# Strided attention on one core: a two-bank normalisation split over three engines, and sums taken one group ahead

## Chip, core, metric

One core of a Trainium2 chip. The metric is the device time of one execution in microseconds (us), the median of several executions. "Span" is the length of the profiled execution; the measured time is about 1.8 us longer. Ratios between kernels are the mean time of one kernel's fast runs over that of the other's of the same rounds, so they are not quite the ratios of the medians that are quoted.

## The reference

Each of 96 heads has 1024 queries of 64 numbers and attends to 16 fixed keys (every 64th position).

```python
for i in range(seq):                                   # cut
    attend_positions = np.arange(0, seq, stride)       # 16 keys
    scores = einsum('bhqd,bhkd->bhqk', q, k) * scale
    weights = np.exp(scores - max); weights /= weights.sum(-1)
    result[:, :, i] = einsum('bhqk,bhkd->bhqd', weights, v)
```

Q is 25 MB in and the result 25 MB out; the arithmetic is small.

## The kernel before

Work goes in 24 groups of 4 heads, 1 MB of Q and 1 MB of output each. GpSimd casts Q to bf16, VectorE transposes it, TensorE makes scores, ScalarE exponentiates them, TensorE makes sums and outputs, VectorE multiplies the outputs by the reciprocal sums, and the DMA queue stores. TensorE's matmuls and VectorE's instructions run in the order of the source, as the trace of before shows (in the group from 72.37 us: sums at 72.37, outputs at 72.87, scores at 73.68, outputs at 74.71). The parts that matter:

```python
def transpose(g):
    nc.vector.transpose(qt[g].bitcast(I32), qb[g].bitcast(I32))

def scores(g):                       # 4 matmuls of 512 columns, then exp
    ...
    for a in range(2):
        nc.scalar.activation(out=..., in_=sc[64*a:64*a+64]..., func=AF.Exp, scale=scale)

def sums(g):                         # 8 weight loads, 8 matmuls of 4 columns
    for i in range(8):
        nc.tensor.matmul(sm[:, :, i], lhsT=wt[g][:, i], rhs=s_sel, ...)
    nc.vector.reciprocal(rec[g], sm...)

def outputs(g, c):                   # c = 0..3: 2 matmuls, one 128x512 multiply
    ...
    nc.vector.tensor_tensor(out=out_sb[g][:, :, 4*c:4*c+4], in0=ps, in1=rec[g]..., op=ALU.mult)

for g in range(NG):
    transpose(g + 2)
    sums(g)
    outputs(g, 0); outputs(g, 1)
    scores(g + 1)
    outputs(g, 2); outputs(g, 3)
    values(g + 2); cast(g + 3)       # GpSimd
    if g in (2, 4): keys(g // 2)     # prepares the keys of 8 more groups
    store(g)
    load(g + 10)
```

Note where the transpose stands: first in group g, for the scores of group g+2, which TensorE reaches only in group g+1.

The softmax here doesn't subtract the row's maximum and nothing guards it: scores larger than these inputs give would overflow.

## Time and profile before

| | before |
|---|---|
| time, median of 4 | 129.65 us |
| VectorE busy | 85% of the span, 97% from 60 us on |
| time per group, steady | 3.97 us |
| DMA | 401 GB/s mean, about 420 in a full stretch |
| last store issued | 120.0 us of 127.7 |

From the page of before: the first line gives the busy time of each engine (PE is TensorE's matmuls, DVE VectorE, ACT ScalarE, POOL GpSimd), the second the busy tenths of the DMA engines in 40 equal slices of the span, the third the volume.

```profile
PE 73.3 (57%) x508; PEld 38.6 (30%) x508; DVE 109.2 (85%) x170; ACT 39.6 (31%) x55; POOL 66.7 (52%) x69
DMA  2999989898998998989989999999999999999981
HBM read 25.95 MB, written 25.17 MB: 400 GB/s over the span
```

From the table of stretches of before: start and end in us, length, busy time (instructions) of each engine, granted TensorE clock (PEclk, the share of full speed that the profile records; 1.00 is full), DMA share, GB/s.

```profile
core 0: us, PE busy (x) PEld busy (x) DVE busy (x) ACT busy (x) POOL busy (x), PEclk, DMA share, GB/s
60.00:70.00 10.00, 5.84 (x55) 3.45 (x55) 9.72 (x17) 4.10 (x6) 7.51 (x6) 1.00 1.01 424
90.00:100.00 10.00, 6.28 (x47) 3.24 (x45) 9.73 (x16) 4.16 (x6) 5.42 (x5) 0.91 1.01 424
```

DMA is full and VectorE is nearly full at once. The groups of instructions of before that VectorE works through (count, total busy us, mean ns of one, idle before and what ended it):

```profile
L254 DVE TENSOR_TENSOR out_sb<-o_ps,rec 128x512 f32<-128x512 f32 x96 | 59.9, 685 | 4.8 <-PE o_ps L249 2.6
L211 DVE STREAM_TRANSPOSE qt<-qb 128x1024 int32<-128x1024 int32 x24 | 29.7, 1237 | 1.6 <-POOL qb L207 1.6
L242 DVE RECIPROCAL rec<-sm 128x32 f32<-128x32 f32 x24 | 7.8, 326 | 0.3 <-PE sm L238 0.3
```

And one group in the timeline of before (start us, duration us, instruction):

```profile
70.55 1.24 DVE L211 STREAM_TRANSPOSE qt<-qb 128x1024 int32<-128x1024 int32 x1
...
71.71 0.32 DVE L242 RECIPROCAL rec<-sm 128x32 f32<-128x32 f32 x1
...
72.12 2.49 DVE L254 TENSOR_TENSOR out_sb<-o_ps,rec 128x512 f32<-128x512 f32 x4
...
73.68 1.24 PE L218 MATMUL sc<-qt,k_t 128*128 128x512 bf16 x4
...
74.52 1.24 DVE L211 STREAM_TRANSPOSE qt<-qb 128x1024 int32<-128x1024 int32 x1
```

VectorE goes from transpose to transpose with hardly a gap in 3.97 us. The transpose ends at 71.79, and the next scores start only at 73.68: those scores don't even use it yet.

### The profile page before, as it was taken

The page shows a single profiled execution, that of the slowest core. Times are in us where ns is not written, and L with a number is a line of the kernel's source. Part 1 is how long each engine was busy: PE and PEld are TensorE (multiplying, and loading weights), DVE is VectorE, ACT ScalarE, POOL GpSimd, SP SyncE. Part 2 cuts the span into 40 slices and gives each one's busy share as a digit, 9 for nine tenths or more (in the row PEclk, how much of TensorE's full clock was granted, in tenths as well). Part 3 has the DMA queues.
Part 4 walks back from the last instruction along what each step waited for, and adds up shares of the span by engine and source line. Part 5 has one row for each costly group of instructions (what it writes and reads, how often), then busy time and mean ns, then how long its engine had stood idle before and what let it go on. Part 6 is the DMA issues. An engine that isn't in the chain of part 4 may idle for free. (4 is left out here: it accounts for less than half of the span.)

```text
span 127.7 us, 1518 instructions
## 1 busy us (share of the span) xinstructions
PE 73.3 (57%) x508; PEld 38.6 (30%) x508; DVE 109.2 (85%) x170; ACT 39.6 (31%) x55; POOL 66.7 (52%) x69
## 2 busy tenths in 40 slices
PE   0006767974476097866675579755567776674000
PEld 0003233441433063333342234432234323342000
DVE  6997468999979987899999999999999999999500
ACT  3003404224244134344424440444431344323000
POOL 8980499675217605387767635787555727000000
PEclk9999999999779855599999965799998559999555
DMA  2999989898998998989989999999999999999981
GB/s 70 380 322 459 482 339 482 349 482 359 462 472 336 503 400 377 505 346 431 493 344 439 454 385 436 441 408 452 426 398 464 385 421 431 426 416 428 421 372 46
DMA packets 7913, 51.23 MB, mean 401 GB/s; under 512 B 3872, under 2 KB 3872, under 8 KB 3872
## 3 DMA queue, kind: packets, MB, share of 16 engines
q1 hardware_dynamic: 7904, 51.12, 96.8%
q8 instruction: 4, 0.07, 0.2%
q14 instruction: 5, 0.04, 0.1%
HBM read 25.95 MB, written 25.17 MB: 400 GB/s over the span
## 5 line engine op out<-in xcount | busy, mean ns | idle before, releaser
L254 DVE TENSOR_TENSOR out_sb<-o_ps,rec 128x512 f32<-128x512 f32 x96 | 59.9, 685 | 4.8 <-PE o_ps L249 2.6
L229 ACT ACTIVATE w<-sc 64x512 bf16<-64x512 f32 x48 | 35.1, 732 | 60.0 <-PE sc L218 56.7
L207 POOL CAST qb<-qn 128x2048 bf16<-128x2048 f32 x24 | 45.5, 1898 | 0.4 <-DMA qn<-in_Q_dram 0.4
L249 PE MATMUL o_ps<-vb,w 128*128 128x256 bf16 x192 | 38.0, 321 | 2.4 <-DVE out_sb L254 1.4
L199 POOL TENSOR_TENSOR vb<-mask,v_rep 128x256 bf16<-128x256 bf16 x24 | 16.1, 670 | 40.3 <-PE o_ps L249 35.4
L218 PE MATMUL sc<-qt,k_t 128*128 128x512 bf16 x96 | 32.7, 472 | 1.5 <-DVE qt L211 1.2
L211 DVE STREAM_TRANSPOSE qt<-qb 128x1024 int32<-128x1024 int32 x24 | 29.7, 1237 | 1.6 <-POOL qb L207 1.6
L249 PEld LDWEIGHTS <-w 128*128 128x128 bf16 x192 | 19.3, 110 | 16.2 <-issue 8.6
L238 PE MATMUL sm<-s_sel,w 128*128 128x4 bf16 x192 | 8.7, 167 | 22.1 <-ACT w L229 22.1
L238 PEld LDWEIGHTS <-w 128*128 128x128 bf16 x192 | 6.9, 100 | 30.1 <-ACT w L229 29.6
L218 PEld LDWEIGHTS <-k_t 128*128 128x128 bf16 x96 | 10.8, 114 | 12.0 <-issue 6.5
L169 PE MATMUL kp<-perm_k,k_m 128*128 128x128 bf16 x24 | 3.1, 311 | 17.5 <-DVE k_m L161 17.5
L242 DVE RECIPROCAL rec<-sm 128x32 f32<-128x32 f32 x24 | 7.8, 326 | 0.3 <-PE sm L238 0.3
L169 PEld LDWEIGHTS <-k_m 128*128 128x128 bf16 x24 | 2.3, 141 | 18.2 <-DVE k_m L161 18.2
L177 ACT CAST k_t<-kp 128x512 bf16<-128x512 f32 x6 | 3.2, 590 | 14.1 <-PE kp L169 14.1
L161 DVE TENSOR_SCALAR k_m<-k_raw,slot_m 128x256 bf16<-128x256 f32 x12 | 6.8, 626 | 0.0
L192 DVE CAST v_rep<-vp 128x384 bf16<-128x384 f32 x4 | 2.2, 558 | 2.6 <-PE vp L188 2.6
L135 POOL MEMSET k_t<- 128x4608 bf16 x1 | 3.9, 3938 | 0.0
L145 DVE TENSOR_SCALAR s_sel<-col,slot_f 128x4 bf16<-128x4 int16 x1 | 3.2, 3155 | 0.1
L188 PE MATMUL vp<-v_bf,perm_v 128*128 128x384 bf16 x4 | 2.0, 489 | 0.8 <-DVE v_rep L192 0.6
L177 ACT ACT_TABLE_LOAD x1 | 1.3, 1283 | 2.1 <-DVE k_t L129 2.1
L129 DVE MEMSET k_t<- 128x1152 uint32 x1 | 1.0, 1018 | 1.0 <-PEq L314 1.0
(17 smaller groups left out, 6.3 us busy)
## 6 DMA issues: line engine op xcount, KB each, us to landing
qn<-in_Q_dram SPq DMA_DIRECT2D x24, 1024.0 KB, 13.9
out_dram<-out_sb SPq DMA_DIRECT2D x24, 1024.0 KB, 12.0
k_raw<-in_K_dram SPq DMA_DIRECT2D x1, 384.0 KB, 4.1
v_raw<-in_V_dram SPq DMA_DIRECT2D x1, 384.0 KB, 7.2
```

The costliest lines, as they stand in the source:

```text
L161: nc.vector.tensor_scalar(out=k_m[:, 4 * m : 4 * m + 4, :, h], in0=kr, scalar1=slot_m[:, h : h + 1], scalar2=None, op0=ALU.mult,)
L169: nc.tensor.matmul(kp[:, i, :, f], lhsT=k_m[:, 4 * m + 2 * u + i, f].rearrange("p h q -> p (h q)"), rhs=perm_k.rearrange("p c a b k -> p c ...
L177: nc.scalar.copy(_ap_with(dst, [dst.ap[0], [KW, 8], [32, 4], [1, NK]], extra_offset=NK), kp.rearrange("p i c f (s k) -> p (i c f) s k", s=4),)
L199: nc.gpsimd.tensor_tensor(out=vb[g], in0=mask, in1=v_rep[:, g // 2, g % 2].unsqueeze(1).to_broadcast([P, 4, D]), op=ALU.mult,)
L207: nc.gpsimd.tensor_copy(out=qb[g], in_=qn[g])
L211: nc.vector.transpose(qt[g].bitcast(I32), qb[g].bitcast(I32))
L218: nc.tensor.matmul(sc, lhsT=k_t[:, g, f, NK * (1 - e) : NK * (1 - e) + P], rhs=_ap_with(q, [q.ap[0], [2 * D, 8], [16 * D, 2], [2, 32]], ex ...
L229: nc.scalar.activation(out=_ap_with(wa, [wa.ap[0], [P, 8], [1, 2], [2, 32]], extra_offset=64 * a), in_=sc[64 * a : 64 * a + 64].rearrange( ...
L238: nc.tensor.matmul(sm[:, :, i], lhsT=wt[g][:, i], rhs=s_sel, start=True, stop=True)
L242: nc.vector.reciprocal(rec[g], sm.rearrange("p b i e -> p b (i e)"))
L249: nc.tensor.matmul(ps[:, :, i], lhsT=wt[g][:, 2 * c + i], rhs=vb[g].rearrange("p s d -> p (s d)"), start=True, stop=True,)
L254: nc.vector.tensor_tensor(out=out_sb[g][:, :, 4 * c : 4 * c + 4], in0=ps.rearrange("p b i (e d) -> p b (i e) d", e=2), in1=rec[g][:, :, 4 ...
```

## The change

The intent: relieve VectorE. Outputs are gathered in tiles of two banks of PSUM (the memory that the matmuls write to), so that one multiply takes 1024 elements; of the other half VectorE takes 512, and ScalarE copies the last quarter to SBUF (the memory of the output tile), where GpSimd scales it. The Q transpose moves from the front of the group to its end, and the scores to its front. The sums are made with fewer instructions (the small selector is the stationary operand, in four column tiles), transposed by VectorE, and taken one group ahead.

```diff
+    def sums_mm(g):
+        for q in range(4):
+            nc.tensor.matmul(sm[32*q:32*q+32], lhsT=sel32,
+                rhs=wt[g][:, :, 32*q:32*q+32], ..., tile_position=(0, 32*q))
+    def sums_rec(g):
+        nc.vector.transpose(smt..., sm...)
+        nc.vector.reciprocal(rec[g], smt[:, :, 0:4])
     def outputs(g, c):              # now c = 0..1, 4 matmuls, no multiply
     ...
+    def normalize(g, c):
+        n = 4 if c == 0 else 2
+        if n < 4:
+            nc.scalar.copy(part(i0 + n, 4 - n), ps[:, n:4])
+        nc.vector.tensor_tensor(out=part(i0, n), in0=ps[:, 0:n], in1=fact(i0, n), op=ALU.mult)
+        if n < 4:
+            nc.gpsimd.tensor_tensor(out=part(i0+n, 4-n), in0=part(i0+n, 4-n), ...)
 ...
     for g in range(NG):
-        transpose(g + 2)
-        sums(g)
+        scores(g + 1)
         outputs(g, 0); outputs(g, 1)
-        scores(g + 1)
-        outputs(g, 2); outputs(g, 3)
+        sums_mm(g + 1)
         values(g + 2); cast(g + 3)
+        normalize(g, 0); normalize(g, 1)
+        sums_rec(g + 1)
+        transpose(g + 2)
         if g in (2, 4): keys(g // 2)
         store(g)
```

(Cut: one output buffer less, the output tiles in PSUM 2 of double size instead of 4, the keys evacuated in one copy instead of two, and the order of rows in the output tile.)

More of the change, by code (lines that the diff above doesn't have):

```diff
@@ L72 @@
     QBUFS = 10
-    OBUFS = 9
+    OBUFS = 8
     const = ctx.enter_context(tc.tile_pool(name="const", bufs=1))
@@ L82 @@
     psum_sc = ctx.enter_context(tc.tile_pool(name="psc", bufs=2, space=bass.MemoryType.PSUM))
-    psum_o = ctx.enter_context(tc.tile_pool(name="po", bufs=4, space=bass.MemoryType.PSUM))
+    psum_o = ctx.enter_context(tc.tile_pool(name="po", bufs=2, space=bass.MemoryType.PSUM))
     psum_s = ctx.enter_context(tc.tile_pool(name="psm", bufs=2, space=bass.MemoryType.PSUM))
@@ L147 @@
     )
+    sel32 = const.tile([P, 32], BF16, name="sel32")
+    nc.vector.memset(sel32, 0.0)
+    nc.vector.tensor_copy(out=sel32[:, 0:4], in_=s_sel)
     slot_m = const.tile([P, 4], FP32, name="slot_m")
@@ L164, in keys @@
             )
-        for u in range(2):
-            kp = psum_o.tile([P, 2, 2, 2, 4 * NK], FP32, name="kp", tag="o")
-            for i in range(2):
-                for f in range(2):
-                    nc.tensor.matmul(
-                        kp[:, i, :, f],
-                        lhsT=k_m[:, 4 * m + 2 * u + i, f].rearrange("p h q -> p (h q)"),
-                        rhs=perm_k.rearrange("p c a b k -> p c (a b k)"),
-                        start=True, stop=True,
-                    )
-            g0 = 8 * m + 4 * u
-            dst = k_t[:, g0 : g0 + 4]
-            nc.scalar.copy(
-                _ap_with(dst, [dst.ap[0], [KW, 8], [32, 4], [1, NK]], extra_offset=NK),
-                kp.rearrange("p i c f (s k) -> p (i c f) s k", s=4),
-            )
+        kp = psum_o.tile([P, 4, 2, 2, 4 * NK], FP32, name="kp", tag="o")
+        for i in range(4):
+            for f in range(2):
+                nc.tensor.matmul(
+                    kp[:, i, :, f],
+                    lhsT=k_m[:, 4 * m + i, f].rearrange("p h q -> p (h q)"),
+                    rhs=perm_k.rearrange("p c a b k -> p c (a b k)"),
+                    start=True, stop=True,
+                )
+        dst = k_t[:, 8 * m : 8 * m + 8]
+        nc.scalar.copy(
+            _ap_with(dst, [dst.ap[0], [KW, 16], [32, 4], [1, NK]], extra_offset=NK),
+            kp.rearrange("p i c f (s k) -> p (i c f) s k", s=4),
+        )
     def value_rows():
@@ L192, in value_rows @@
                 nc.vector.tensor_copy(out=v_rep[:, 6 * n : 6 * n + 6, c], in_=vp)
-    qb, qt, wt, vb, rec, out_sb = {}, {}, {}, {}, {}, {}
+    qb, qt, wt, vb, rec, out_sb, o_ps, sm_ps = {}, {}, {}, {}, {}, {}, {}, {}
     def values(g):
@@ L220, in scores @@
                     rhs=_ap_with(
-                        q, [q.ap[0], [2 * D, 8], [16 * D, 2], [2, 32]],
-                        extra_offset=D * e + f,
+                        q, [q.ap[0], [D, 8], [16 * D, 2], [2, 32]],
+                        extra_offset=8 * D * e + f,
                     ),
@@ L233, in scores @@
             )
-    def sums(g):
-        sm = psum_s.tile([P, 2, 8, 2], FP32, name="sm", tag="sm")
-        for i in range(8):
+    def sums_mm(g):
+        sm = sm_ps[g] = psum_s.tile([P, 8, 32], FP32, name="sm", tag="sm")
+        for q in range(4):
             nc.tensor.matmul(
-                sm[:, :, i], lhsT=wt[g][:, i], rhs=s_sel, start=True, stop=True
-            )
-        rec[g] = rec_pool.tile([P, 2, 16], FP32, name="rec", tag="rec")
-        nc.vector.reciprocal(rec[g], sm.rearrange("p b i e -> p b (i e)"))
+                sm[32 * q : 32 * q + 32], lhsT=sel32,
+                rhs=wt[g][:, :, 32 * q : 32 * q + 32],
+                start=True, stop=True, tile_position=(0, 32 * q),
+            )
+    def sums_rec(g):
+        sm = sm_ps[g]
+        smt = rec_pool.tile([P, 8, 32], FP32, name="smt", tag="smt")
+        nc.vector.transpose(
+            smt.rearrange("p i r -> p (i r)"), sm.rearrange("p i r -> p (i r)")
+        )
+        rec[g] = rec_pool.tile([P, 8, 4], FP32, name="rec", tag="rec")
+        nc.vector.reciprocal(rec[g], smt[:, :, 0:4])
     def outputs(g, c):
         if c == 0:
-            out_sb[g] = out_pool.tile([P, 2, 16, D], FP32, name="out_sb", tag="out_sb")
-        ps = psum_o.tile([P, 2, 2, 2 * D], FP32, name="o_ps", tag="o")
-        for i in range(2):
+            out_sb[g] = out_pool.tile([P, 4, 8, D], FP32, name="out_sb", tag="out_sb")
+        ps = psum_o.tile([P, 4, 4, D], FP32, name="o_ps", tag="o")
+        o_ps[g, c] = ps
+        for i in range(4):
             nc.tensor.matmul(
-                ps[:, :, i], lhsT=wt[g][:, 2 * c + i],
+                ps[:, i].rearrange("p s d -> p (s d)"), lhsT=wt[g][:, 4 * c + i],
                 rhs=vb[g].rearrange("p s d -> p (s d)"),
@@ L253, in outputs @@
             )
+    def normalize(g, c):
+        ps = o_ps[g, c]
+        i0 = 4 * c
+        n = 4 if c == 0 else 2
+        part = lambda k, m: out_sb[g][:, :, k : k + m].rearrange("p s i d -> p i s d")
+        fact = lambda k, m: rec[g][:, k : k + m].unsqueeze(3).to_broadcast([P, m, 4, D])
+        if n < 4:
+            nc.scalar.copy(part(i0 + n, 4 - n), ps[:, n:4])
         nc.vector.tensor_tensor(
-            out=out_sb[g][:, :, 4 * c : 4 * c + 4],
-            in0=ps.rearrange("p b i (e d) -> p b (i e) d", e=2),
-            in1=rec[g][:, :, 4 * c : 4 * c + 4].unsqueeze(3).to_broadcast([P, 2, 4, D]),
-            op=ALU.mult,
-        )
+            out=part(i0, n), in0=ps[:, 0:n], in1=fact(i0, n), op=ALU.mult
+        )
+        if n < 4:
+            nc.gpsimd.tensor_tensor(
+                out=part(i0 + n, 4 - n), in0=part(i0 + n, 4 - n),
+                in1=fact(i0 + n, 4 - n), op=ALU.mult,
+            )
     def store(g):
@@ L276 @@
     transpose(1)
+    sums_mm(0)
+    sums_rec(0)
     values(1)
@@ L279 @@
     for g in range(NG):
-        if g + 2 < NG:
-            transpose(g + 2)
-        sums(g)
+        if g + 1 < NG:
+            scores(g + 1)
         outputs(g, 0)
@@ L285 @@
         if g + 1 < NG:
-            scores(g + 1)
-        outputs(g, 2)
-        outputs(g, 3)
+            sums_mm(g + 1)
         if g + 2 < NG:
@@ L292 @@
             cast(g + 3)
+        normalize(g, 0)
+        normalize(g, 1)
+        if g + 1 < NG:
+            sums_rec(g + 1)
+        if g + 2 < NG:
+            transpose(g + 2)
         if g in (2, 4):
```

## The prediction

> **What bounds the kernel now.** Two limits nearly meet. The page's DMA line shows the DMA engines full from 5 us to 124 us (51.2 MB, about 420 GB/s in steady stretches). A load plus a store (2.1 MB) costs 5.0 us at that rate, a store alone 2.5. VectorE is 97% busy in the table of stretches from 60 us on; the timeline gives one group (transpose 1.24 us, reciprocal 0.33, four 128x512 multiplies 2.48) every 3.97 us. The last store is issued at 120.0 us with only some 0.9 MB queued before it, so VectorE and DMA end together.
>
> **The work.** VectorE per group, estimated from those durations (512 elements 0.53 us, fixed part 0.15, overlap 0.06): a 128x1024 multiply 1.16 us, a 128x512 one 0.63, sums transpose of 256 elements about 0.42, reciprocal 0.33, Q transpose 1.24: 3.8 us against 3.97, only 4% less. ScalarE gains a 128x512 copy (0.6 us, beside 1.5 of exp). GpSimd gains a 128x512 fp32 multiply, about 1.25 us (estimated from the 128x256 one, 0.67), making 3.8. Sums fall from 8 weight loads and matmuls to 4. DMA bytes do not change.
>
> **The order; this decides.** Before, the Q transpose stood first in a group and was used a whole group later. Now transpose(g+2) is VectorE's last work of group g, and scores(g+2) is TensorE's first of group g+1, ahead of the outputs that VectorE's next multiply needs. The trace of before shows both engines keeping source order[...]. So each group is a closed ring: transpose, 4 score matmuls, 4 output matmuls, two multiplies, sums transpose, reciprocal, transpose. VectorE idles for the TensorE part. From the timeline: at the fast matmul pace 0.05 + 0.87 + 0.60 + 0.05 = 1.6 us; at the slow pace (scores 1.71, outputs 1.05) 2.9. Ring: about 5.45 us fast, 6.7 slow. Both exceed DMA's 5.0, so this ring binds.
>
> [...] In before, TensorE changed pace several times at about 50% busy. After, it would be some 40% busy at the fast pace, so I expect it to alternate, ring about 6.1 us.
>
> **Sum.** First store about 23.8 us (before 23.6); 22 rings of 6.1 = 134; last group without transpose or scores 2.6; two key preparations 3.2 each = 6.4; last store alone with the end 5.5; measured time over span 1.9. Total about 174 us. All fast: 160; all slow: 188.
>
> Predicted time 173 us, range 157 to 187. Chances: faster by over 2% 0.04, within 2% 0.04, slower by over 2% 0.92.
>
> **What would show each step right.** Stores issued 5.4 to 6.7 us apart instead of 4.0. VectorE idle before the 128x1024 multiply 1.6 to 2.9 us a group, released by the output matmuls; scores waiting for the Q transpose in nearly every group. VectorE busy 60 to 65% of the span. DMA about 300 GB/s mean. The chain of waits alternating between VectorE and TensorE over the whole span. GpSimd's new multiply near 1.25 us, off the chain.
>
> **What would make it wrong.** If transposes in fact came early enough for the scores, the kernel would stay at DMA's limit, 127 to 130 us. If TensorE stayed fast, 160; if slow, 188. If ScalarE's copy or GpSimd's multiply into the shared output tile were serialised with VectorE's, add up to 0.7 us a group.

That the pace would alternate, and the ring be about 6.1 us, is the author's estimate from before, where the granted clock changed between 1.00 and 0.50 nine times from 33.4 to 118.7 us, with TensorE 57% busy over the span. The split of a multiply into 0.53 us for 512 elements and a fixed part of 0.15 was an estimate too: before shows only the 685 ns of one, and 2.49 us for four in a row. After measured 1224 ns for 1024 elements and 691 for 512, so 0.53 and 0.16.

## The result

| | before | after |
|---|---|---|
| time, median of 4 | 129.65 us | 191.3 us (190.56 to 192.65) |
| ratio of the fast runs | 1 | 1.476, 95% interval 1.467 to 1.485 |
| VectorE busy | 109.2 us, 85% | 106.5 us, 56% |
| time per group, steady | 3.97 us | 6.83 us |
| DMA mean | 401 GB/s | 270 GB/s |

From the page of after: engines, DMA in 40 slices, volume, and the chain of work that ended last by engine.

```profile
PE 95.1 (50%) x412; PEld 46.8 (25%) x412; DVE 106.5 (56%) x148; ACT 53.7 (28%) x76; POOL 91.8 (48%) x93
DMA  5999999996579097796799689775514522531546
HBM read 25.95 MB, written 25.17 MB: 270 GB/s over the span
PE 40%; DVE 38%; ACT 12%; issue 4%; POOL 1%; DVEq 1%; ACTq 0%
```

No engine is near full, and DMA starves. The chain (the work that each step waited for, followed back from the end) now alternates between TensorE and VectorE, with ScalarE's copy between them. The waits of after (who waited for whom: total us, times, longest):

```profile
DVE out_sb L276 <- PE o_ps L262: 65.6, 23, 3.7
PE sc L220 <- DVE qt L213: 62.2, 21, 3.0
...
DVE out_sb L276 <- ACT out_sb L275: 2.8, 15, 0.2
```

VectorE waits 2.85 us a group (65.6 over 23) for outputs, and TensorE waits 2.96 us a group (62.2 over 21) for the Q transpose: each stands still while the other works. The durations of the new instructions, the first two lines from the groups of after with the shapes kept apart, the others from its page:

```profile
L276 DVE TENSOR_TENSOR out_sb<-o_ps,rec 128x1024 f32<-128x1024 f32 x24 | 29.4, 1224 | 65.7 <-PE o_ps L262 65.6
L276 DVE TENSOR_TENSOR out_sb<-o_ps,rec 128x512 f32<-128x512 f32 x24 | 16.6, 691 | 3.7 <-ACT out_sb L275 2.8
```

```profile
L280 POOL TENSOR_TENSOR out_sb<-out_sb,rec 128x512 f32<-128x512 f32 x24 | 25.0, 1042 | 64.2 <-ACT out_sb L275 64.2
L249 DVE STREAM_TRANSPOSE smt<-sm 128x256 f32<-128x256 f32 x24 | 10.5, 438 | 0.0
```

One group in the timeline of after, from scores to scores:

```profile
100.87 1.86 PE L220 MATMUL sc<-qt,k_t 128*128 128x512 bf16 x4 [3.03 <-DVE qt L213]
...
102.53 1.81 PE L262 MATMUL o_ps<-vb,w 128*128 128x256 bf16 x8
...
102.83 1.50 ACT L231 ACTIVATE w<-sc 64x512 bf16<-64x512 f32 x2 [4.65 <-PE sc L220]
103.62 1.22 DVE L276 TENSOR_TENSOR out_sb<-o_ps,rec 128x1024 f32<-128x1024 f32 x1 [2.81 <-PE o_ps L262]
...
104.42 0.59 ACT L275 COPY out_sb<-o_ps 128x512 f32<-128x512 f32 x1
...
105.04 0.69 DVE L276 TENSOR_TENSOR out_sb<-o_ps,rec 128x512 f32<-128x512 f32 x1 [0.19 <-ACT out_sb L275]
...
105.64 0.44 DVE L249 STREAM_TRANSPOSE smt<-sm 128x256 f32<-128x256 f32 x1
...
106.19 0.35 DVE L253 RECIPROCAL rec<-smt 128x32 f32<-128x32 f32 x1
106.46 1.19 DVE L213 STREAM_TRANSPOSE qt<-qb 128x1024 int32<-128x1024 int32 x1
...
107.70 1.87 PE L220 MATMUL sc<-qt,k_t 128*128 128x512 bf16 x4 [3.04 <-DVE qt L213]
```

This is a ring: each step waits for the one before it, and the first scores wait for the last step of the group before. Follow it once round. Scores to the start of exp 1.96 us; exp 1.50; gap and copy 0.09 + 0.59; second multiply to the end of the Q transpose 0.03 + 2.61; to the next scores 0.05. That makes 6.83 us, the whole group. The copy waits for the outputs too, which end at 104.34, 0.01 us after exp. So two paths are nearly tied here, and the page's chain takes the one through the outputs (15% of the span, exp 4%). The first multiply is not quite on either path: it ended at 104.84, and the second could have started then, but waited 0.19 us for ScalarE's copy.

Last, the pace of TensorE in one group, from the table of stretches of after for TensorE alone (start and end, length, busy, granted clock, DMA share, GB/s):

```profile
122.20:123.20 1.00, 1.00 (x4) 0.50 1.18 352
123.20:124.20 1.00, 1.00 (x7) 0.50 1.00 238
124.20:125.20 1.00, 0.95 (x8) 0.81 1.12 459
125.20:126.20 1.00, 0.00 (x0) 1.00 1.21 524
126.20:127.20 1.00, 0.00 (x0) 1.00 0.01 0
127.20:128.20 1.00, 0.02 (x1) 0.90 0.33 139
128.20:129.20 1.00, 1.00 (x3) 0.50 1.12 467
```

The full clock is granted from about 124.6 to 128.0 us, when TensorE has only the end of the outputs and the sums left, until 125.15, and then nothing to do. When it makes scores and nearly all of the outputs, the clock is at half.

### The profile page after: what moved, and what is told of

Its sections match the earlier page's. It is cut to its first block, busy times and chain, and to the rows that moved or that the text cites. A ratio compares the mean times of both kernels' runs of the same rounds, so it can differ in the third digit from the quotient of the medians.

```text
span 189.4 us, 1405 instructions
## 1 busy us (share of the span) xinstructions
PE 95.1 (50%) x412; PEld 46.8 (25%) x412; DVE 106.5 (56%) x148; ACT 53.7 (28%) x76; POOL 91.8 (48%) x93
## 4 chain that ended last, share of the span: by engine, by line
PE 40%; DVE 38%; ACT 12%; issue 4%; POOL 1%; DVEq 1%; ACTq 0%
PE sc L220 24%; PE o_ps L262 15%; DVE qt L213 12%; DVE out_sb L276 9%; ACT out_sb L275 7%; DVE smt L249 4%; DVE rec L253 4%; DVE k_m L165 4%; ACT w L231 4%; DVE s_sel L146 2%; PE kp L172 2%; POOL qb L209 1%; DVE w L134 1%; ACT k_t L179 1%; DVE k_t L130 1%
## 5 line engine op out<-in xcount | busy, mean ns | idle before, releaser
L276 DVE TENSOR_TENSOR out_sb<-o_ps,rec 128x1024 f32<-128x1024 f32 (+1 forms) x48 | 45.9, 958 | 69.4 <-PE o_ps L262 65.6
L220 PE MATMUL sc<-qt,k_t 128*128 128x512 bf16 x96 | 44.9, 618 | 63.3 <-DVE qt L213 62.2
L280 POOL TENSOR_TENSOR out_sb<-out_sb,rec 128x512 f32<-128x512 f32 x24 | 25.0, 1042 | 64.2 <-ACT out_sb L275 64.2
L262 PE MATMUL o_ps<-vb,w 128*128 128x256 bf16 x192 | 42.3, 396 | 0.5 <-DVE out_sb L276 0.5
L275 ACT COPY out_sb<-o_ps 128x512 f32<-128x512 f32 x24 | 14.1, 586 | 3.1 <-PE o_ps L262 1.5
L249 DVE STREAM_TRANSPOSE smt<-sm 128x256 f32<-128x256 f32 x24 | 10.5, 438 | 0.0
L240 PE MATMUL sm<-w,sel 128*32 128x256 bf16 x96 | 9.9, 284 | 0.0
L253 DVE RECIPROCAL rec<-smt 128x32 f32<-128x32 f32 x24 | 8.5, 353 | 2.3
L179 ACT CAST k_t<-kp 128x1024 bf16<-128x1024 f32 x3 | 3.0, 1012 | 21.1 <-PE kp L172 21.1
L240 PEld LDWEIGHTS <-sel 128*32 128x32 bf16 x96 | 4.5, 92 | 8.2 <-issue 7.5
```

Of the source, the lines that this page charges most:

```text
L220: nc.tensor.matmul(sc, lhsT=k_t[:, g, f, NK * (1 - e) : NK * (1 - e) + P], rhs=_ap_with(q, [q.ap[0], [D, 8], [16 * D, 2], [2, 32]], extra_ ...
L249: nc.vector.transpose(smt.rearrange("p i r -> p (i r)"), sm.rearrange("p i r -> p (i r)"))
L253: nc.vector.reciprocal(rec[g], smt[:, :, 0:4])
L262: nc.tensor.matmul(ps[:, i].rearrange("p s d -> p (s d)"), lhsT=wt[g][:, 4 * c + i], rhs=vb[g].rearrange("p s d -> p (s d)"), start=True, ...
L275: nc.scalar.copy(part(i0 + n, 4 - n), ps[:, n:4])
L276: nc.vector.tensor_tensor(out=part(i0, n), in0=ps[:, 0:n], in1=fact(i0, n), op=ALU.mult)
```

## The experiments

Theory: a closed ring of dependencies, made by the order of the source, sets the group's time; the new instructions themselves are not to blame. Rival: the split work costs the time (contention, slow GpSimd, tiling). A second question was why the ring came out at 6.83 us rather than 6.1. Eight kernels ran; all were correct. The first four ran on one chip, the other four on another, each set beside the kernel before (129.86 and 129.81 us).

### transpose_first

```diff
+        transpose(g + 2)
         normalize(g, 0); normalize(g, 1)
         sums_rec(g + 1)
-        transpose(g + 2)
```

> The change, with one move: the Q transpose of group g+2 stands before the two multiplies of group g on VectorE instead of after the sums; every instruction is kept. Theory (closed ring transpose, scores, outputs, multiplies): the transpose is then ready a whole group before its scores, VectorE no longer waits 2.8 us per group, stores come about 4 us apart as long as VectorE binds, and the time falls to DMA's limit, 127 to 133 us. Rival (the parts themselves cost the time: two-bank multiply, ScalarE copy, GpSimd multiply, column-tiled sums): the time stays near 190 us.

Measured: 131.76 us, ratio to before 1.017 (1.0135 to 1.0209), so a little slower than before. One moved instruction takes back 59.5 of the 61.6 us. The groups follow each other every 3.61 us, less than the 3.97 of before, so the split does relieve VectorE. The rival falls: every new instruction is still there. In the table of stretches of transpose_first:

```profile
core 0: us, PE busy (x) PEld busy (x) DVE busy (x) ACT busy (x) POOL busy (x), PEclk, DMA share, GB/s
60.00:65.00 5.00, 4.10 (x26) 2.06 (x27) 4.79 (x9) 3.35 (x5) 5.00 (x6) 1.00 0.82 342
...
80.00:90.00 10.00, 7.62 (x44) 3.53 (x44) 9.69 (x15) 5.41 (x9) 9.86 (x10) 1.00 1.00 423
```

VectorE and GpSimd are both full now (9.69 and 9.86 of 10 us), and DMA has one stretch at 342 GB/s. Why the kernel is nevertheless not faster than before is left to early_loads.

### outputs_first

```diff
-        scores(g + 1)
         outputs(g, 0); outputs(g, 1)
+        scores(g + 1)
         sums_mm(g + 1)
```

> The change, with one move: on TensorE the output matmuls of group g stand before the score matmuls of group g+1. Everything else, the late transpose too, is kept. Theory A, as the prediction worded it (VectorE waits because the outputs stand behind the scores): the 2.8 us wait for the outputs vanishes and the time falls far, to 130 to 145 us. Theory B (the late transpose closes more than one ring: transpose, scores, exp, ScalarE copy, second multiply, and transpose, scores, exp, sums, sums transpose are nearly as long): VectorE's wait only moves from the outputs to the copy or the sums, the ring stays at 6.6 to 6.9 us, and the time stays at 185 to 193 us.

Measured: 193.38 us, 1.489 times before, 0.4 us above the range of theory B. Theory B holds: the wait of VectorE for the outputs is gone, and nearly the same wait stands elsewhere, now for ScalarE's copy (waits of outputs_first):

```profile
DVE out_sb L276 <- ACT out_sb L275: 68.8, 23, 4.0
```

The ring is 6.75 us, with scores of 1.86 or 1.87 us, the slow pace, in every group from 69.3 us to the end (mean granted clock 0.587). ScalarE's copy of group g stands behind the exp of group g+1, and that exp needs the late transpose. So it is not the place of the scores ahead of the outputs that closes the ring, as the prediction worded it.

### vector_first

```diff
-        nc.scalar.copy(part(...), ps[:, n:4])        # if n < 4
         nc.vector.tensor_tensor(out=part(i0, n), ...)
+        nc.scalar.copy(part(...), ps[:, n:4])        # if n < 4
```

> The change, with VectorE's 128x512 multiply written ahead of ScalarE's copy, so that it no longer waits 0.2 us for that copy. Theory of fixed durations: the ring falls from 6.83 to 6.63 us, the time by 22 x 0.2 = 4.4 us to about 187 us. Theory of the lock (the ring of 6.83 us is two of the 3.41 us steps in which TensorE's pace changes, and settles on them): the ring stays at 6.83 us and the time at 191 us within 1 us.

Measured: 184.16 us, 1.420 times before. This was a test of my own suspicion: 6.83 us is just twice the 3.41 us after which TensorE's clock changes in the trace of after (0.50 from 121.18 to 124.59 us, 1.00 to 128.00, 0.50 to 131.41). As a cause of the length the suspicion fell: most rings are now 6.55 us, 0.28 us shorter, and a few are 5.3 to 6.4 where the fast pace met the scores. The two multiplies now take 1.82 us together instead of 2.11: beside the wait of 0.19 they gain 0.09 by following each other directly. The time fell 7 us, more than the 4.4 expected. The run does not exclude that the ring of after, within its last 0.1 us, keeps step with the clock: from 94 to 176 us its twelve rings last 81.93 us, 6.83 each, the length of two steps, while the earlier ones without key preparation are 6.64 to 6.84.

### keep_busy

```diff
+    spare = psum_d.tile([P, 4 * D], FP32, name="spare")     # sums buffers 2 -> 1
+    def fill(n):
+        for _ in range(n):
+            nc.tensor.matmul(spare, lhsT=identity, rhs=mask..., start=True, stop=True)
 ...
+            fill(4)
             sums_mm(g + 1)
+            fill(14)
```

> The change, plus 18 spare matmuls of 256 columns in each group (4 before the sums, 14 after) into a PSUM bank that nobody reads, and one sums buffer instead of two. Question: is the missing term of my sum TensorE's slow pace? Theory: TensorE stays at the fast pace, scores take 1.03 instead of 1.86 us and outputs start 0.85 us sooner; the ring then runs through exp, the ScalarE copy and the second multiply and falls to about 6.0 us, the time to about 172 us (165 to 177). If the pace is not what was mis-sized, the time stays at 191 us or rises by the spare work.

Measured: 174.01 us, 1.341 times before, with a mean granted clock of 0.957 against 0.766. Doing more work on TensorE made the kernel 17 us faster, because most scores now meet the fast pace (1.06 us instead of 1.86). The ring is 5.96 us, and VectorE waits in it for the copy (waits of keep_busy):

```profile
DVE out_sb L285 <- PE o_ps L271: 40.8, 24, 3.7
...
DVE out_sb L285 <- ACT out_sb L284: 11.4, 23, 0.5
```

### before_late_transpose

Nothing of the change but its order (scores first, transpose last), on the kernel before:

```diff
     for g in range(NG):
-        transpose(g + 2)
+        scores(g + 1)
         sums(g)
         outputs(g, 0); outputs(g, 1)
-        scores(g + 1)
         outputs(g, 2); outputs(g, 3)
         values(g + 2); cast(g + 3)
+        transpose(g + 2)
```

> The kernel before, with nothing of the change but its order: scores of group g+1 first on TensorE, the Q transpose of group g+2 last on VectorE. Four 128x512 multiplies, eight sums matmuls, no ScalarE copy, no GpSimd multiply. Theory (order alone): a ring transpose, scores, sums, reciprocal, four multiplies, transpose: 4.0 us of VectorE work plus 0.05 + 1.96 + 0.4 slow or 0.05 + 1.1 + 0.35 fast, so 5.5 to 6.4 us a group, time 155 to 182 us, and no gain over the change larger than that. Rival (the parts cost the time): stays at 130 us within 3%.

Measured: 173.48 us (three fast runs, 171.79 to 174.29, and one slow), 1.332 times before by the fast runs. The order alone costs about 43 us, with the old instructions. VectorE waits for the sums now (waits of before_late_transpose), and most groups take 6.23 us:

```profile
DVE rec L242 <- PE sm L238: 47.9, 23, 3.0
```

### keep_busy_vector_first

Both edits of keep_busy and vector_first.

> The change with both: 18 spare matmuls a group, and VectorE's second multiply ahead of ScalarE's copy. keep_busy alone gave a ring of 5.96 us with 0.54 us of VectorE's wait on the copy; taking that wait away should give the ring that I had summed for the fast pace, 5.4 to 5.5 us, and 162 us (159 to 165). If some other wait stands right behind the copy, the ring stays at 5.8 us or more and the time over 169 us.

Measured: 163.38 us, 1.258 times before; the ring is 5.33 us. This is the ring that the prediction had summed for the fast pace (5.45 us); it exists, but only with both the pace and the copy out of the way.

### outputs_and_vector_first

Both edits of outputs_first and vector_first.

> The change with both moves: outputs ahead of the scores on TensorE, and VectorE's second multiply ahead of ScalarE's copy. Neither the outputs nor the copy can hold VectorE then. If the late transpose also closes a ring through exp and the sums (transpose, scores 1.96, exp 1.49, last sums 0.45, then sums transpose to Q transpose 2.0, waits 0.1: 6.0 us slow, about 5.1 fast), VectorE waits for the sums instead and the time is 168 to 175 us. If no third ring exists, VectorE's 3.6 us of work bind, and the time falls to 130 us.

Measured: 171.5 us, 1.323 times before. VectorE's wait moved once more, to the sums (waits of outputs_and_vector_first); the rings are 5.99 us at the slow pace and 5.2 at the fast one:

```profile
DVE smt L249 <- PE sm L240: 46.3, 23, 2.9
```

### early_loads

transpose_first, with loads two groups further ahead and not behind the store:

```diff
+    load(QBUFS); load(QBUFS + 1)          # ahead of the loop
     ...
+        load(g + QBUFS + 2)
         store(g)
-        load(g + QBUFS)
```

> The transpose_first version, with the loads issued two groups further ahead and before the store of the group, so that a store that waits for its group does not hold a load. transpose_first had 3.61 us a group and yet 131.8 us, with DMA at 342 GB/s between 60 and 65 us, after the key preparations had held the stores 9.5 us. Theory (DMA ran dry there): DMA stays full, the time falls by 1 to 2 us below transpose_first and by 0 to 1.5% below the kernel before: 127.5 to 130 us. Rival (DMA's rate, not its queue, was lower): no gain, 131 to 132 us.

Measured: 129.67 us, 0.999 times before (0.9975 to 1.0001). The stretch from 60 to 65 us is full now (table of stretches of early_loads):

```profile
60.00:65.00 5.00, 4.08 (x27) 2.05 (x27) 4.79 (x9) 3.20 (x5) 5.00 (x6) 1.00 1.03 436
```

The last multiply is over at 116.8 us and the DMA engines work on at about 420 GB/s until 124. The relief of VectorE is real and worth nothing here: DMA needs about 122 us for its 51.1 MB at 420 GB/s (an estimate from these two figures) whatever VectorE does. None of the versions beats the kernel before; this one equals it.

## Why the prediction was right in kind and wrong in size

- **Direction and mechanism: right.** The late transpose closes a ring through VectorE and TensorE, longer than DMA's 5.0 us a group. Shown by transpose_first (moving it back gives 131.76 us) and by before_late_transpose (in the kernel before, moving it to the end and the scores to the front gives 173.48 us).
- **"ahead of the outputs that VectorE's next multiply needs": too narrow.** outputs_first and outputs_and_vector_first showed two more rings, through exp and the copy (6.75 us) and through exp and the sums (5.99 us slow). Of the moves tried, only that of the transpose opens all three.
- **The step that failed: "so I expect it to alternate, ring about 6.1 us".** TensorE's pace does alternate, but within every group, and the scores of the profiled run met the slow pace in every group: 1.86 to 1.91 us each time, rings of 6.64 us at first and 6.83 from 80 us on. One ring at the slow pace stood where the average of two was expected. The fast stretch fell on TensorE's idle time. 22 rings x (6.83 - 6.1) = 16 us, nearly all of the 18.3 us by which 173 was short. keep_busy shows that the pace is the cause: with a mean clock of 0.957 and scores of 1.06 us, 174.01 us. (That this is near the 173 predicted is luck: its ring of 5.96 us runs through the copy at the fast pace, where 5.45 and 160 us were predicted.) And the mean clock says nothing by itself: the four runs of after had mean clocks of 0.766, 0.766, 0.655 and 0.607 at 191.12, 191.47, 192.65 and 190.56 us. In the profiled runs what counts is the clock at the instructions on the ring (scores 1.86 us at 0.50 in after, 1.06 us at 1.00 in transpose_first); the three runs of after without a trace can't be read so.
- **The ring lengths themselves: close.** Slow 6.7 predicted, 6.83 measured, of which 0.28 go with the wait for ScalarE's copy (6.55 in vector_first). Fast 5.45 predicted, 5.33 measured in keep_busy_vector_first. The copy's wait, named as a risk of up to 0.7 us, was real.
- **The range: a fault of bookkeeping.** My own all-slow case was 188 us, above the upper end of 187 that I gave. I trusted an average over two paces that I had not placed in the group.
- **The smaller terms of the sum:** first store 24.5 us (predicted 23.8); a group with key preparation 10.28 us, so 3.45 above a ring (predicted 3.2). Together about 1.2 us too little.
- **Signs named ahead:** stores came 6.83 us apart, just outside the 5.4 to 6.7 predicted. VectorE's wait 2.85 us a group (1.6 to 2.9 predicted), scores waiting in 21 groups, the chain alternating: seen. VectorE busy 56% (60 to 65) and DMA 270 GB/s (about 300) follow from the longer span. GpSimd's multiply took 1.04 us (1.25), off the ring.

Why the fast stretch fell on TensorE's idle half can be read from the traces in part, though no run varied it on purpose. In before and after, each stretch between two changes of the clock lasts 3.41 us or a multiple of it (up to 20.48 us in before, one or two steps in after). In after, TensorE was busy 3.24 of the 3.41 us of the step to 124.59 us and got the full clock in the next; there it was busy 0.56 us, and got half in the one after, to 131.41 us. A ring of 6.83 us is two such steps, so in after the full clock comes each time one step too late. In before the clock fell at 74.4 us, after a stretch in which TensorE was 55% busy (table of stretches of before for TensorE alone; length, busy, clock):

```profile
71.00:74.40 3.40, 1.86 (x18) 0.99 1.11 467
74.40:78.00 3.60, 2.81 (x19) 0.50 0.98 412
```

About the same busy share stood beside either pace: in before the clock was 0.50 from 74.4 to 78.0 us with TensorE 78% busy, in transpose_first it was 1.00 from 80 to 90 us with 76%. In outputs_first TensorE was busy about 69% of a ring (scores 1.87, sums 0.80 and outputs 2.01 of 6.75 us), and its scores kept the slow pace from 69.3 us to the end.

Left open: what sets the clock, which these runs do not show (the ends of matmuls are modelled in a trace, too); and how the pace lay in the runs without a trace.

## What to carry to other kernels

When work is moved between engines, draw the ring before adding up busy times: what does the last instruction of a group on one engine release, and does that engine's next instruction depend on it? An instruction whose result is wanted a group later belongs at the front of the group; moved to the end, it cost more here than all the saved work (191.3 us against 131.76). If such a ring contains matmuls, sum it with the slow pace too: the fast pace fell on TensorE's idle part in after (scores 1.86 us in every ring), and stayed away in outputs_first (1.87 us from 69.3 us on). And where DMA was full already, the relieved engine gained nothing (early_loads, 129.67 us against 129.81).
